# Prefix log-sum-exp: single-row-block tiles at the two ends of the run, each in a loop of its own

## The chip, the cores and the metric

The kernel runs on one core of one Trainium2 chip. The metric is the device time of that core in microseconds, the median of several runs. A ratio is the mean time of one kernel's runs over that of the kernel before in the same rounds, so it is not quite the ratio of the medians quoted beside it.

## The reference

```python
def reference(x):                       # x: (4, 4096, 4128) float32
    out = np.zeros_like(x)
    out[:, 0, :] = x[:, 0, :].copy()
    for t in range(1, S):
        mx = np.maximum(out[:, t - 1, :], x[:, t, :])
        out[:, t, :] = mx + np.log(np.exp(out[:, t - 1, :] - mx) + np.exp(x[:, t, :] - mx))
    return out.astype(np.float32)
```

It is a running log-sum-exp along the second axis. The kernel computes it as Ln of a running sum of Exp.

## The kernel before

A **block** is 128 rows of 4128 columns, 2.114 MB. Each batch has 32 blocks. A **step** loads up to R = 3 blocks into one of four buffers, sums them in place and stores them from the same buffer. `b` counts the batches.

```python
    steps = []
    for b in range(B):
        n = S // P
        parts = [R] * (n // R) + ([n % R] if n % R else [])
        if b == 0:
            parts.reverse()
        # ... one Step per entry of parts

    chunks = [Chunk(s, c) for s in steps for c in range(n_main)]
    ahead = bufs - 1
    for s in steps[:ahead]:
        s.load()
```

Each step is four chunks of 1024 columns. For each chunk ScalarE (ACT) takes Exp, VectorE (DVE) adds the blocks of the step to each other (`own`), TensorE multiplies by a triangular matrix for the rows above (`head`), VectorE adds that from PSUM (`add_above`), TensorE carries the last row on (`pick`), and ScalarE takes Ln. One software-pipelined loop goes over all chunks of all steps; the Exp runs two chunks ahead, across the border between steps:

```python
    chunks[0].act(ACT.Exp)
    chunks[1].act(ACT.Exp)
    # ...
    for g, k in enumerate(chunks):
        if g + 1 < len(chunks):
            chunks[g + 1].own()
            chunks[g + 1].head()
        if g + 2 < len(chunks):
            chunks[g + 2].act(ACT.Exp)
        if g:
            finish(chunks[g - 1])
            result(chunks[g - 1])      # Ln; after the last chunk: store, and load step stored+3
        k.add_above()
        # ... pick
```

The softmax here doesn't subtract the row's maximum and nothing guards it: scores larger than these inputs give would overflow.

Of the kernel before, what the change touches and what calls it, by code (L numbers as in the profile page):

```python
# [1 line left out]

# [4 lines left out]

FP32 = mybir.dt.float32
ACT = mybir.ActivationFunctionType
P = 128  # L10
R = 3
CH = 1024
MM = 512


def _constants(nc, pool):

    excl = pool.tile([P, P], FP32, name="excl")
    nc.gpsimd.memset(excl, 1.0)  # L19

    nc.gpsimd.affine_select(  # L21
        out=excl, in_=excl, pattern=[[1, P]], compare_op=mybir.AluOpType.is_ge,
        fill=0.0, base=-1, channel_multiplier=-1,
    )
    pick = pool.tile([P, P], FP32, name="pick")
    nc.gpsimd.memset(pick, 0.0)  # L26
    nc.gpsimd.affine_select(  # L27
        out=pick, in_=pick, pattern=[[0, P]], compare_op=mybir.AluOpType.not_equal,
        fill=1.0, base=-(P - 1), channel_multiplier=1,
    )  # L30
    return excl, pick


@with_exitstack
def kernel(
    ctx: ExitStack,
    tc: tile.TileContext,
    x: bass.AP,
    out: bass.AP,
):  # L40







    nc = tc.nc
    B, S, D = x.shape
    assert S % P == 0  # L50
    n_main = D // CH
    tail = D - n_main * CH
    t0 = n_main * CH
    last = n_main - 1

    nc.scalar.preload_act_table_set("natural_log_exp_and_others")  # L56
    consts = ctx.enter_context(tc.tile_pool(name="consts", bufs=1))
    excl, pick = _constants(nc, consts)

    bufs = 4  # L60
    xpool = ctx.enter_context(tc.tile_pool(name="xpool", bufs=bufs))
    cpool = ctx.enter_context(tc.tile_pool(name="cpool", bufs=1))
    psum = ctx.enter_context(tc.tile_pool(name="psum", bufs=1, space=bass.MemoryType.PSUM))

    above = [psum.tile([P, CH], FP32, name=f"above{c}") for c in range(n_main)]

    above_t = above[last][:, CH - MM:CH - MM + tail]
    carry_t = cpool.tile([P, tail], FP32, name="carry_t")
    nc.vector.memset(carry_t, 0.0)  # L69

    ctx.enter_context(tc.manual_schedule())

    def mm(pt, w, rhs, start=False, stop=False):
        nc.tensor.matmul(pt, lhsT=w, rhs=rhs, start=start, stop=stop, skip_group_check=True)  # L74

    def add(o, a, b):
        nc.vector.tensor_tensor(out=o, in0=a, in1=b, op=mybir.AluOpType.add)  # L77

    class Step:


        def __init__(self, b, row, r):
            self.b, self.row, self.r = b, row, r
            self.first = row == 0
            self.final = row + P * r == S

        def dram(self, t):
            rows = t[self.b, self.row:self.row + P * self.r, :]
            return rows.rearrange("(p j) d -> p j d", j=self.r)

        def load(self):
            full = xpool.tile([P, R, D], FP32, name="xt")
            self.xt = full[:, :self.r, :]
            nc.sync.dma_start(out=self.xt, in_=self.dram(x))  # L94

        def store(self):
            nc.sync.dma_start(out=self.dram(out), in_=self.xt)  # L97

    class Chunk:
        def __init__(self, step, c):  # L100
            self.t, self.c = step, c
            self.a, self.b = c * CH, D if c == last else (c + 1) * CH

        def act(self, func):
            v = self.t.xt[:, :, self.a:self.b]
            nc.scalar.activation(v, v, func)  # L106

        def own(self):

            x = self.t.xt  # L110
            for j in range(1, self.t.r):
                v = x[:, j, self.a:self.b]
                add(v, x[:, j - 1, self.a:self.b], v)

        def head(self):

            t, a = self.t, self.a
            for s in range(0, CH, MM):
                mm(above[self.c][:, s:s + MM], excl, t.xt[:, t.r - 1, a + s:a + s + MM],
                   start=t.first, stop=True)  # L120

        def add_above(self):
            t, a = self.t, self.a
            v = t.xt[:, :, a:a + CH]
            add(v, v, above[self.c].unsqueeze(1).to_broadcast([P, t.r, CH]))

        def pick(self, s0=0, s1=CH):

            t, a = self.t, self.a
            if not t.final:  # L130
                for s in range(s0, s1, MM):
                    mm(above[self.c][:, s:s + MM], pick, t.xt[:, t.r - 1, a + s:a + s + MM],
                       start=True)

        def tail_head(self):
            t = self.t
            if not t.first:
                mm(above_t, pick, carry_t, start=True)
            mm(above_t, excl, t.xt[:, t.r - 1, t0:D], start=t.first, stop=True)

        def tail_add(self):
            t = self.t
            v = t.xt[:, :, t0:D]
            add(v, v, above_t.unsqueeze(1).to_broadcast([P, t.r, tail]))
            if not t.final:
                nc.vector.tensor_copy(carry_t[96:, :], t.xt[96:, t.r - 1, t0:D])  # L146

    steps = []
    for b in range(B):
        n = S // P  # L150
        parts = [R] * (n // R) + ([n % R] if n % R else [])
        if b == 0:
            parts.reverse()
        row = 0
        for r in parts:
            steps.append(Step(b, row, r))
            row += P * r
        assert row == S

    chunks = [Chunk(s, c) for s in steps for c in range(n_main)]  # L160
    ahead = bufs - 1
    for s in steps[:ahead]:
        s.load()
    stored = 0
    def finish(k):
        if k.c == last:
            k.tail_add()
            k.pick(CH - MM)

    def result(k):  # L170
        nonlocal stored
        k.act(ACT.Ln)
        if k.c == last:
            k.t.store()
            if stored + ahead < len(steps):
                steps[stored + ahead].load()
            stored += 1

    chunks[0].act(ACT.Exp)
    chunks[1].act(ACT.Exp)  # L180
    chunks[0].own()
    chunks[0].head()
    for g, k in enumerate(chunks):
        if g + 1 < len(chunks):
            chunks[g + 1].own()
            chunks[g + 1].head()
        if g + 2 < len(chunks):
            chunks[g + 2].act(ACT.Exp)
        if g:
            finish(chunks[g - 1])  # L190
            result(chunks[g - 1])
        k.add_above()
        if k.c == last:
            k.tail_head()
            k.pick(0, CH - MM)
        else:
            k.pick()
    finish(chunks[-1])
    result(chunks[-1])


# [1 line left out]
_INS = ['x']  # L203
_OUTS = [((4, 4096, 4128), 'float32')]


# [23 lines left out]
```

## Time and profile before

| | before |
|---|---|
| median time | 1265.1 us (4 runs, 1263.9 to 1265.9) |
| span of the profiled run | 1266.3 us |
| steps, loads, stores | 44, 44, 44 |
| bytes moved | 541.07 MB: 256 blocks, 128 in and 128 out |
| DMA queue / DVE / ACT / PE busy | 99.3% / 77% / 73% / 60% |

The page gives each engine's busy time and share, then strips of 40 equal slices; in the DMA strip a 9 is 90% or more. The prediction below shows the page's lines, the start of the queue and single transfers. Two more lines of the kernel before matter, from the timeline of its end. The columns are start, length of the merged group, engine, line, operation, data, count, and the idle time ahead of it with its cause.

```profile
1218.60 33.39 SPq L97 DMA_DIRECT2D out_dram<-xt  x3
1226.15 20.85 ACT L106 ACTIVATE xt<-xt 128x2048 f32<-128x2048 f32 x10 [2.19 <-DMA xt<-in_x_dram]
```

The last three stores go out between 1218.6 and 1252. From 1226 us on ACT has the four Exps of the last step, with three Lns of the step before it between them, and then three of the last step's own Lns, ten in one unbroken run: that is the streaming which the change gives up at the ends.

### The profile page before, as it was taken

The numbers are of one execution on the slowest core, as the hardware profiler recorded it, in microseconds if no ns is written. First come the engines' busy times: TensorE is split into PE (matmuls) and PEld (weight loads), VectorE is DVE, ScalarE is ACT, GpSimd is POOL, SyncE is SP. The second block draws the span as 40 slices with busy tenths as digits, with TensorE's granted clock in tenths as the row PEclk, the third lists the DMA queues.
The fourth block names the chain that finished last, engine by engine and source line by source line (L and its number), as shares of the span: only waits on it lengthen the run. The fifth ranks groups of instructions, "written<-read, shape, count | busy, mean of one in ns | idle before, by whom it ended". The sixth has DMA issues, their size and how long they took to land.

```text
span 1266.3 us, 4623 instructions
## 1 busy us (share of the span) xinstructions
PE 760.5 (60%) x1512; PEld 289.0 (23%) x1512; DVE 980.6 (77%) x597; ACT 923.8 (73%) x353; POOL 1.1 (0%) x8
## 2 busy tenths in 40 slices
PE   4676665555666666666366666665646656666562
PEld 1222222222222222222122222222212222222220
DVE  3998777777777878788579878777857978787793
ACT  4887666777777777767668777666866877766794
POOL 0000000000000000000000000000000000000000
PEclk9998888887788888888779888888877988888886
DMA  9999999999999999999999999999999999999998
GB/s 409 384 425 424 427 429 443 426 427 440 432 429 441 426 430 440 429 431 433 434 434 434 429 440 430 431 437 433 432 419 434 426 433 433 431 432 438 426 418 349
DMA packets 12695, 541.35 MB, mean 427 GB/s; under 512 B 1409, under 2 KB 1409, under 8 KB 1409
## 3 DMA queue, kind: packets, MB, share of 16 engines
q1 hardware_dynamic: 12672, 541.07, 99.3%
q8 instruction: 12, 0.20, 0.1%
q14 instruction: 11, 0.08, 0.0%
HBM read 270.53 MB, written 270.53 MB: 427 GB/s over the span
## 4 chain that ended last, share of the span: by engine, by line
DMA 67%; DVE 12%; ACT 9%; PE 8%; issue 1%; SPq 0%; ACTq 0%
DMA xt<-in_x_dram 63%; DVE xt L77 12%; ACT xt L106 9%; PE above L74 8%; DMA out_dram<-xt 5%; SPq L97 0%; ACTq L106 0%; SPq L94 0%; DVE carry_t L146 0%
## 5 line engine op out<-in xcount | busy, mean ns | idle before, releaser
L106 ACT ACTIVATE xt<-xt 128x3072 f32<-128x3072 f32 (+2 forms) x352 | 922.5, 2693 | 327.0 <-DMA xt<-in_x_dram 290.5
L74 PE MATMUL above<-xt,excl 128*128 128x512 f32 (+1 forms) x792 | 443.1, 687 | 348.7 <-DVE xt L77 339.4
L77 DVE TENSOR_TENSOR xt<-xt 128x1024 f32<-128x1024 f32 (+1 forms) x336 | 413.4, 1230 | 255.0 <-ACT xt L106 249.4
L77 DVE TENSOR_TENSOR xt<-xt,above 128x3072 f32<-128x3072 f32 (+3 forms) x220 | 582.9, 2651 | 11.7 <-PE above L74 10.3
L74 PE MATMUL above<-xt,pick 128*128 128x512 f32 x640 | 330.7, 630 | 130.0 <-DVE xt L77 130.0
L74 PEld LDWEIGHTS above<-xt,excl 128*128 128x128 f32 x792 | 162.6, 229 | 601.5 <-issue 490.5
L74 PEld LDWEIGHTS above<-xt,pick 128*128 128x128 f32 x640 | 113.6, 198 | 307.4 <-DVE xt L77 227.2
L74 PEld LDWEIGHTS above<-carry_t,pick 128*128 128x128 f32 x80 | 20.8, 271 | 51.4 <-DVE xt L77 48.2
L74 PE MATMUL above<-carry_t,pick 128*128 128x32 f32 x80 | 17.5, 308 | 10.1 <-DVE xt L77 10.1
L146 DVE COPY carry_t<-xt 32x32 f32<-32x32 f32 x40 | 7.1, 178 | 1.4
L56 ACT ACT_TABLE_LOAD x1 | 1.3, 1283 | 0.8 <-PEq L214 0.8
L69 DVE MEMSET carry_t<- 128x32 f32 x1 | 0.1, 85 | 0.9 <-PEq L214 0.9
L27 POOL TENSOR_SCALAR_AFFINE_SELECT pick<-pick 128x128 f32<-128x128 f32 x1 | 0.3, 293 | 0.0
L21 POOL TENSOR_SCALAR_AFFINE_SELECT excl<-excl 128x128 f32<-128x128 f32 x1 | 0.3, 292 | 0.0
L19 POOL MEMSET excl<- 128x128 f32 x1 | 0.2, 204 | 0.3 <-POOLq L214 0.3
L26 POOL MEMSET pick<- 128x128 f32 x1 | 0.2, 204 | 0.0
L214 POOL MEMSET const-bfloat16-1.0<- 128x1 bf16 x1 | 0.1, 101 | 0.0
L214 POOL MEMSET const-uint8-127<- 128x1 uint8 x1 | 0.1, 101 | 0.0
L214 POOL MEMSET const-float32-0.0<- 128x1 f32 x1 | 0.1, 98 | 0.3 <-issue 0.3
L214 POOL MEMSET const-float32-1.0<- 128x1 f32 x1 | 0.1, 98 | 0.0
## 6 DMA issues: line engine op xcount, KB each, us to landing
xt<-in_x_dram SPq DMA_DIRECT2D x40, 6192.0 KB, 41.1
out_dram<-xt SPq DMA_DIRECT2D x40, 6192.0 KB, 27.0
xt<-in_x_dram SPq DMA_DIRECT2D x4, 4128.0 KB, 36.2
out_dram<-xt SPq DMA_DIRECT2D x4, 4128.0 KB, 19.6
```

Of the source, the lines that this page charges most:

```text
L19: nc.gpsimd.memset(excl, 1.0)
L21: nc.gpsimd.affine_select(out=excl, in_=excl, pattern=[[1, P]], compare_op=mybir.AluOpType.is_ge, fill=0.0, base=-1, channel_multiplier=-1,)
L26: nc.gpsimd.memset(pick, 0.0)
L27: nc.gpsimd.affine_select(out=pick, in_=pick, pattern=[[0, P]], compare_op=mybir.AluOpType.not_equal, fill=1.0, base=-(P - 1), channel_mul ...
L56: nc.scalar.preload_act_table_set("natural_log_exp_and_others")
L69: nc.vector.memset(carry_t, 0.0)
L74: nc.tensor.matmul(pt, lhsT=w, rhs=rhs, start=start, stop=stop, skip_group_check=True)
L77: nc.vector.tensor_tensor(out=o, in0=a, in1=b, op=mybir.AluOpType.add)
L106: nc.scalar.activation(v, v, func)
L146: nc.vector.tensor_copy(carry_t[96:, :], t.xt[96:, t.r - 1, t0:D])
L214: nc = _bacc.Bacc("TRN2", target_bir_lowering=False, num_devices=1)
```

## The change

The intent is to let the run begin and end with a small tile: one block first, one block last, with the first and last step in loops of their own. The first batch becomes 1, 3x10, 1 (it was 2, 3x10), and the last 3x10, 1, 1 (it was 3x10, 2).

```diff
-        parts = [R] * (n // R) + ([n % R] if n % R else [])
-        if b == 0:
-            parts.reverse()
+
+        parts = [R] * (n // R)
+        if b == 0 and n % R:
+            parts = [1] + parts + [1] * (n % R - 1)
+        elif b == B - 1:
+            parts = parts + [1] * (n % R)
+        elif n % R:
+            parts = parts + [n % R]
...
-    chunks = [Chunk(s, c) for s in steps for c in range(n_main)]
...
+    for part in (steps[:1], steps[1:-1], steps[-1:]):
+        chunks = [Chunk(s, c) for s in part for c in range(n_main)]
+        # the same loop body as before, one level deeper
```

More of the change, by code (lines that the diff above doesn't have):

```diff
@@ L177, in result @@
             stored += 1
-    chunks[0].act(ACT.Exp)
-    chunks[1].act(ACT.Exp)
-    chunks[0].own()
-    chunks[0].head()
-    for g, k in enumerate(chunks):
-        if g + 1 < len(chunks):
-            chunks[g + 1].own()
-            chunks[g + 1].head()
-        if g + 2 < len(chunks):
-            chunks[g + 2].act(ACT.Exp)
-        if g:
-            finish(chunks[g - 1])
-            result(chunks[g - 1])
-        k.add_above()
-        if k.c == last:
-            k.tail_head()
-            k.pick(0, CH - MM)
-        else:
-            k.pick()
-    finish(chunks[-1])
-    result(chunks[-1])
+    for part in (steps[:1], steps[1:-1], steps[-1:]):
+        chunks = [Chunk(s, c) for s in part for c in range(n_main)]
+        chunks[0].act(ACT.Exp)
+        chunks[1].act(ACT.Exp)
+        chunks[0].own()
+        chunks[0].head()
+        for g, k in enumerate(chunks):
+            if g + 1 < len(chunks):
+                chunks[g + 1].own()
+                chunks[g + 1].head()
+            if g + 2 < len(chunks):
+                chunks[g + 2].act(ACT.Exp)
+            if g:
+                finish(chunks[g - 1])
+                result(chunks[g - 1])
+            k.add_above()
+            if k.c == last:
+                k.tail_head()
+                k.pick(0, CH - MM)
+            else:
+                k.pick()
+        finish(chunks[-1])
+        result(chunks[-1])
 _INS = ['x']
```

## The prediction

> **What bounds the kernel now.** I read the page first (strips, queue share), then the SyncE timeline, then the issue view one transfer at a time.
>
> ```profile
> span 1266.3 us, 4623 instructions
> PE 760.5 (60%) x1512; PEld 289.0 (23%) x1512; DVE 980.6 (77%) x597; ACT 923.8 (73%) x353; POOL 1.1 (0%) x8
> DMA  9999999999999999999999999999999999999998
> GB/s 409 384 425 424 427 429 443 426 427 440 432 429 441 426 430 440 429 431 433 434 434 434 429 440 430 431 437 433 432 419 434 426 433 433 431 432 438 426 418 349
> q1 hardware_dynamic: 12672, 541.07, 99.3%
> ```
>
> The transfers are the bound: one queue is busy 99.3% of the span, while the busiest engine, DVE, has 77%. The strip of GB/s sags only in the first two slices and the last: a few us are all that ordering can win.
>
> ```profile
> 0.80 1.33 SPq L94 DMA_DIRECT2D xt<-in_x_dram  x3
> 42.64 0.35 SPq L97 DMA_DIRECT2D out_dram<-xt  x1
> 43.03 0.43 SPq L94 DMA_DIRECT2D xt<-in_x_dram  x1
> 68.38 0.34 SPq L97 DMA_DIRECT2D out_dram<-xt  x1
> 68.82 0.38 SPq L94 DMA_DIRECT2D xt<-in_x_dram  x1
> 92.60 0.34 SPq L97 DMA_DIRECT2D out_dram<-xt  x1
> ```
>
> These are the issues at the start: three loads at once, then a store and a load per step (a store at L97 waits for the step's last Ln). The next lines are answers of the issue view for single transfers: the first store, then the first full-size store and load after it.
>
> ```profile
> out_dram<-xt SPq DMA_DIRECT2D x1, 4128.0 KB, 12.2
> out_dram<-xt SPq DMA_DIRECT2D x1, 6192.0 KB, 17.9
> xt<-in_x_dram SPq DMA_DIRECT2D x1, 6192.0 KB, 34.3
> ```
>
> Issue plus time to landing gives a chain of landings. The first loads land at 13.1, 27.7 and 42.5 us, so three row blocks cost 14.65 us, **one block 4.88 us**, if the queue is never dry. The first store is issued at 42.64, when the last of those loads has just landed, and takes 12.2 instead of 2 x 4.88 = 9.8: **a dry queue costs about 2.4 us**. The load behind it lands at 69.5 (14.7 later, no loss), the second store at 86.3 and its load at 103.1 (16.8 each: 2.1 lost twice, as the store came at 68.38, only 1.1 us before the queue ran dry). From the fifth store on, stores come every 29.4 us and a load lands 41.5 us after issue: at each store some 12 us of work is queued. A load's landing is followed 16.9 us later by the store of the step before it (landing 1201.7, store 1218.6). At the end the last two stores are issued at 1239.7 and 1251.65 and land at 1255.7 and 1265.6; the transfer before them landed at 1240.7, so the end loses less than 1 us now.
>
> **What the Trainium skill says.**
> - "DMA: Bandwidth & Descriptors", section Bandwidth, gives a fabric ceiling of 435 GB/s for a core's 16 engines. A block is 2.114 MB, so 4.88 us is 433 GB/s: the trace agrees, and there is no faster steady state to reach.
> - Same page, "Anatomy of one DMA": about 2.0 us fixed per transfer (fitted on the GpSimd path), mostly the receipt of the last byte. The 2.4 us of a dry queue agrees; it is hidden while others are queued.
> - "TensorE: Matmul & The Clock Gate", Part 1: the array runs at half clock until about 3.4 us of activity. The first matmuls here step at 0.85 us against 0.43 later: the trace agrees.
> - Same page, queue depths: ScalarE and VectorE are strict FIFO. Hence an Exp of the next step that waits for its load holds back the Ln of this one; the first ACT wait at 27.7 us shows it.
>
> **The change part by part.**
>
> Steps: before 2,3x10 | 3x10,2 | 3x10,2 | 3x10,2 (44). After 1,3x10,1 | 3x10,2 | 3x10,2 | 3x10,1,1 (46). Bytes are the same; four more transfers of 4.88 us, hidden when queued. The first and last step are each their own loop, so the engines fill and drain there.
>
> *Start.* Three loads now bring 7 blocks, landing at 8.2, 22.9 and 37.6 us (3.35 us of lead-in from 13.1 - 9.8, then 4.88 per block). Step 0 alone: an Exp of 1024 columns is about 0.98 us (1.90 for 2048 and 2.75 for 3072 give 0.85 per 1024), an add with PSUM 1.22 (3.35 and 2.28 give 1.07 per 1024). TensorE orders it: four heads and four picks of four 0.43 us passes, 8 x 1.72 = 13.8, plus 1.7 cold and 0.9 for the tail: from 9.2 to 25.5, Ln to about 26.5. So store 0 and load 3 go out at 26.5, 16 us sooner, with the queue still full: **the dry spot at 42.6 goes away** (-2.4). Load 3 lands at 37.6 + 4.9 + 14.65 = 57.2.
>
> Then the catch. Step 1 starts on ACT at 26.5 instead of 27.7: Exp 2.75, two own-sums of 2.5 each with the second hidden behind a cold head of 3.4, so its first add with PSUM is near 35 instead of 37.98. From that add to the store it was 68.38 - 37.98 = 30.4, four DVE rounds of 5.66 and the tail, so store 1 comes at **about 65**, only 3.4 us sooner, while the queue ran dry at 57.2, 12.3 us sooner than 69.5. Store 1 lands at 65 + 2.4 + 14.65 = 82 with 14 blocks done; before, 86.3 with 16. Two blocks are 9.8: **5.5 us behind**. Starting from a really dry queue, the load behind may not lose its 2.1 again, so I count 4.5.
>
> *Middle.* The 1-block step at the end of batch 0 makes one supply 4 blocks (19.5 us) where stores come 29.3 apart, so the backlog falls from 12 to 12.4 + 19.5 - 29.3 = 2.6 us once, and once more when that step is stored. The old 2-block steps fall to 7.6 and lose nothing. At a backlog of 1.1 a loss of 2.1 was seen, at 2.6 I count **1 us** in all.
>
> *End.* Count from the store that issues the last 3-block load (before: 1159.86, span ends 105.7 later). Backlog 12.4 + 29.3 = 41.7. The next store at 29.2 adds 3 + 1 blocks, to 61.2; the next at 41.7 + 16.7 = 58.4 adds 3 + 1, to 80.7. The last 3-block store follows some 20.5 us later (21.1 before), at 79, to 95.4; the next-to-last block about 10 later (6 PE passes of 1.72 groups, tail, Ln), at 89, to 100.3. Only then does the last step begin its Exp: 0.98 + four heads 6.9 + add 1.2 + tail 1.2 + Ln 1.0 = 11.5 and up to 1.7 more if the PE clock has dropped: store at 101.5 to 103. The queue is dry at 100.3, so it lands at 102 + 2.4 + 4.9 = 109.5 instead of 105.7: **about 4 us behind**. Its data had landed at 80.7, so that is the cost of not streaming.
>
> *Sum.* 1265.8 + 4.5 + 1 + 4 = about 1275; I say 1274, as some of the dry spots overlap with receipts already paid.
>
> **The rivals.**
> 1. *The short ends win as intended.* A smaller first load and last store shorten fill and drain: -2.4 at the start, and a last store of 1 block instead of 2 saves 4.9 if nothing else binds: about 1259. For: the low first and last slices. Against: at the end the queue is already nearly full up to the last byte, and fewer blocks in the first three loads leave less to do until store 1, which DVE sets.
> 2. *All is hidden:* the backlog of 12 us swallows both, 1264 to 1268. For: 99.3% busy. Against: no backlog exists near the start and end.
> 3. *The drains hit in full:* fill and drain of engines, some 17 us each, appear whole in the span, 1290 to 1300. For: step 1's Exp stands behind step 0's last Ln. Against: its data lands only 3.6 us before that Ln ends, and the queue holds work through both.
>
> **Range and chances.** Rival 1 sets the low side only partly; the restarts at low backlog (0 to 2 us each, four places) the high side: 1266 to 1282. Faster by 2% needs under 1240.5, while 256 blocks at 4.88 are 1249 alone: 1%. Slower by 2% needs over 1291: only rival 3, 3%. Within 2%: 96%.
>
> **What would show it.** First store near 26.5, second near 65 with a gap in transfers between about 57 and 66; no gap at 42; last store issued some 12 us after the one before, behind a short gap; GB/s of slice 2 below 384, steady slices unchanged near 432; DVE and ACT busy up by a few us. I am wrong if store 1 comes before 60, if the last store is issued within 10 us of the one before it, or if steady slices change.

## The result

The changed kernel takes **1279.8 us** in the median (4 runs, 1277.8 to 1282.4) against 1265.1, a ratio of 1.0118 (95% interval 1.0097 to 1.0139): 14.7 us slower, within the 2% that counts as the same. From the page of its profile:

```profile
span 1280.6 us, 4817 instructions
PE 787.9 (62%) x1584; PEld 302.5 (24%) x1584; DVE 973.8 (76%) x601; ACT 926.8 (72%) x369; POOL 1.1 (0%) x8
DMA  9799999999999999999999999999999999999998
GB/s 413 314 395 420 424 441 429 436 426 413 415 418 421 421 443 423 443 423 438 432 431 438 426 443 424 439 427 438 431 421 431 435 421 432 435 432 435 432 381 373
q1 hardware_dynamic: 13248, 541.07, 98.6%
```

The bytes are the same and no engine's work grew by more than PE's 27 us (72 matmuls more, for two steps more). The new spots are slices 2 and 3, with 314 and 395 GB/s instead of 384 and 425, slices 10 to 14 (the end of the first batch), with 413 to 421 instead of 426 to 441, and slice 39, with 381 instead of 418. The SyncE timeline of the start, as the prediction shows it of before:

```profile
0.80 1.33 SPq L94 DMA_DIRECT2D xt<-in_x_dram  x3
28.36 0.35 SPq L97 DMA_DIRECT2D out_dram<-xt  x1
28.75 0.43 SPq L94 DMA_DIRECT2D xt<-in_x_dram  x1
66.11 0.34 SPq L97 DMA_DIRECT2D out_dram<-xt  x1
66.55 0.38 SPq L94 DMA_DIRECT2D xt<-in_x_dram  x1
90.94 0.34 SPq L97 DMA_DIRECT2D out_dram<-xt  x1
```

The first store comes 14 us sooner (28.4 for 42.6), the second only 2.3 us sooner (66.1 for 68.4). In between, 11 blocks were all that the queue was given. The stretches view of those us (window, length, busy us and instructions of PE, PEld, DVE, ACT and POOL, the granted PE clock, the DMA share, GB/s) shows the hole:

```profile
58.50:66.50 8.00, 5.73 (x13) 1.87 (x12) 7.87 (x8) 4.40 (x3) 0.00 (x0) 1.00 0.00 0
```

For 8 us no transfer moves a byte, and DVE is busy for 7.87 of them: it works on step 1. The issue view of the second store and of the load behind it gives the landings, 83.1 and 101.2 us:

```profile
out_dram<-xt SPq DMA_DIRECT2D x1, 6192.0 KB, 17.0
xt<-in_x_dram SPq DMA_DIRECT2D x1, 6192.0 KB, 34.6
```

Three blocks cost 14.65 us in a full queue. The store takes 17.0, so 2.4 more; the load lands 18.1 after it, so 3.4 more again. What holds step 1 is seen in the timeline of the start:

```profile
27.26 11.78 ACT L106 ACTIVATE xt<-xt 128x1056 f32<-128x1056 f32 x5 [1.48 <-PE above L74]
31.02 2.48 DVE L77 TENSOR_TENSOR xt<-xt 128x1024 f32<-128x1024 f32 x2 [4.82 <-ACT xt L106]
37.40 3.35 DVE L77 TENSOR_TENSOR xt<-xt,above 128x3072 f32<-128x3072 f32 x1 [1.24 <-PE above L74]
```

The group at 27.26 begins with the last Ln of step 0, and the first Exp of step 1 follows it, although its data landed at 23 us. DVE's first add for step 1 is at 37.40, against 37.98 before.

To add up the whole run I use one measure: the **lateness** of a landing, its time minus 4.883 us (14.65 / 3) for each block landed until then (issue time plus time to landing, for each transfer). A full queue keeps it nearly constant; any dry spot raises it. Both profiled runs are 2.6 to 3.0 us above their kernel's median, so their difference can stand for that of the medians.

| at | before | after | difference | grown there |
|---|---|---|---|---|
| load 4 landed (19 and 17 blocks) | 103.1 - 92.8 = 10.3 | 101.2 - 83.0 = 18.2 | 7.9 | start 7.9 |
| 88 blocks | 442.1 - 429.7 = 12.4 | 453.3 - 429.7 = 23.6 | 11.2 | end of batch 0: 3.3 |
| last load landed (248 and 251 blocks) | 1226.1 - 1211.0 = 15.1 | 1253.7 - 1225.6 = 28.1 | 13.0 | rest of the middle: 1.8, of it 0.9 at the last load |
| last store landed (256) | 1265.5 - 1250.0 = 15.5 | 1279.5 - 1250.0 = 29.5 | 14.0 | end 1.0 |

One profile each is a thin base for such a split. Of the kernels below, end-only and doubled begin exactly as the kernel before, and stand at 8.9 and 8.6 at load 4, where it has 10.3; start-only and removed begin as the changed one, and stand at 16.1 and 16.8 where it has 18.2. So the start costs some 6 to 9 us; the means, 17.0 and 9.3, give 7.7.

Over half of the loss is in the first 100 us and little at the end, where the new serial step is plain to see in the timeline:

```profile
1250.48 23.11 SPq L97 DMA_DIRECT2D out_dram<-xt  x3
1258.91 4.89 ACT L106 ACTIVATE xt<-xt 128x1056 f32<-128x1056 f32 x5 [1.70 <-PE above L74]
1260.99 8.83 PE L74 MATMUL above<-xt,excl 128*128 128x512 f32 x16 [2.17 <-ACT xt L106]
1272.15 1.08 ACT L106 ACTIVATE xt<-xt 128x1056 f32<-128x1056 f32 x1 [1.63 <-DVE xt L77]
```

The last step's Exps stand behind the Ln of the step before it at 1258.9, and its last Ln ends at 1273.2. The store before it goes out at 1260.0 and lands at 1273.3, the last one goes out at 1273.3 and lands at 1279.5. The 13.3 us of serial work on the last step are hidden by the transfers that are still queued; only the 1.4 us by which the last landing exceeds a block's 4.9 are open.

### The profile page after: what moved, and what is told of

Its sections match the earlier page's. It is cut to its first block, busy times and chain, and to the rows that moved or that the text cites. A ratio compares the mean times of both kernels' runs of the same rounds, so it can differ in the third digit from the quotient of the medians.

```text
span 1280.6 us, 4817 instructions
## 1 busy us (share of the span) xinstructions
PE 787.9 (62%) x1584; PEld 302.5 (24%) x1584; DVE 973.8 (76%) x601; ACT 926.8 (72%) x369; POOL 1.1 (0%) x8
## 4 chain that ended last, share of the span: by engine, by line
DMA 64%; DVE 13%; PE 13%; ACT 8%; issue 1%; SPq 0%; ACTq 0%; DVEq 0%
DMA xt<-in_x_dram 61%; DVE xt L77 13%; PE above L74 13%; ACT xt L106 8%; DMA out_dram<-xt 4%; SPq L97 0%; DVE carry_t L146 0%; ACTq L106 0%; SPq L94 0%; DVEq L77 0%
## 5 line engine op out<-in xcount | busy, mean ns | idle before, releaser
L106 ACT ACTIVATE xt<-xt 128x3072 f32<-128x3072 f32 (+4 forms) x368 | 925.5, 2585 | 345.6 <-DMA xt<-in_x_dram 277.6
L74 PE MATMUL above<-xt,excl 128*128 128x512 f32 (+1 forms) x828 | 454.2, 676 | 336.6 <-DVE xt L77 307.9
L77 DVE TENSOR_TENSOR xt<-xt,above 128x3072 f32<-128x3072 f32 (+4 forms) x230 | 584.4, 2543 | 52.8 <-PE above L74 51.4
L77 DVE TENSOR_TENSOR xt<-xt 128x1024 f32<-128x1024 f32 (+1 forms) x328 | 403.7, 1231 | 243.2 <-ACT xt L106 237.7
L74 PE MATMUL above<-xt,pick 128*128 128x512 f32 x672 | 348.4, 632 | 137.4 <-DVE xt L77 137.4
L74 PEld LDWEIGHTS above<-xt,excl 128*128 128x128 f32 x828 | 169.9, 228 | 597.1 <-issue 489.6
L74 PEld LDWEIGHTS above<-xt,pick 128*128 128x128 f32 x672 | 119.0, 197 | 320.8 <-DVE xt L77 236.9
L74 PE MATMUL above<-carry_t,pick 128*128 128x32 f32 x84 | 18.2, 306 | 9.9 <-DVE xt L77 9.9
```

Source lines behind the costliest of these rows:

```text
L74: nc.tensor.matmul(pt, lhsT=w, rhs=rhs, start=start, stop=stop, skip_group_check=True)
L77: nc.vector.tensor_tensor(out=o, in0=a, in1=b, op=mybir.AluOpType.add)
L106: nc.scalar.activation(v, v, func)
```

## The experiments

**Theory A:** a store that comes after the queue has run dry is what costs. At the start there are too few blocks to last until store 1; in the middle a single-block step supplies too little; at the end the last step is serial. **Theory B:** the drains of the engines between the three loops cost. Two finer rivals come up below: **B2**, that the serial last step is the greater part, and **F**, that the late landings in the middle are instruction fetches. Kernels sent together shared the chip and the runs of the kernel before, whose median was 1264.6 to 1264.8 us; each experiment has 4 to 6 runs.

### Row blocks only

```diff
+        parts = [R] * (n // R)
+        if b == 0 and n % R:
+            parts = [1] + parts + [1] * (n % R - 1)
+        elif b == B - 1:
+            parts = parts + [1] * (n % R)
+        elif n % R:
+            parts = parts + [n % R]
     # the single streamed loop of the kernel before
```

> The new row blocks (1, 3x10, 1 in the first batch; 3x10, 1, 1 in the last), but one streamed loop over all steps as in the kernel before. Theory A (too few blocks at the start, single-block steps in the middle that let the queue run low, and a serial last step): only the fill of step 1 and the last step get better than in the changed kernel, so store 1 comes near 63.5 us instead of 66.1, its transfer still waits in a queue dry since 58, the middle loses its 5 us as before, and the end loses under 1 us. About 10 us over the kernel before, some 1275 us, ratio 1.007 to 1.010. Theory B (the split of the loop is the cost): within 3 us of the kernel before, ratio under 1.003.

Measured: 1277.4 us, ratio 1.0100 (1.0085 to 1.0116), at the upper edge of what Theory A said. The SyncE timeline of its start:

```profile
38.06 0.35 SPq L97 DMA_DIRECT2D out_dram<-xt  x1
63.38 0.34 SPq L97 DMA_DIRECT2D out_dram<-xt  x1
```

Store 1 comes at 63.4, where Theory A put it at 63.5. Load 3 had landed at 60.0; store 1 lands 5.8 us late. After 20 blocks the lateness is 14.5, against 10.4 before (after 22 blocks) and 18.1 in the changed kernel (after 20): the blocks alone bring 4.1 of the start's loss. The middle loses what it lost in the changed kernel: 1.7 us at load 12 and 1.6 at load 15. At the end, streamed here, the last store loses nothing. Theory B, which allowed a ratio under 1.003, falls.

### Split only

```diff
+    for part in (steps[:1], steps[1:-1], steps[-1:]):
     # the row blocks of the kernel before: 2, 3x10 | 3x10, 2 | ...
```

> The row blocks of the kernel before (2 first, 2 last), but the first and last step each in a loop of their own. Theory A: store 0 near 35 us with the queue still full, store 1 near 73 instead of 68.4, into a queue dry since 67; the last store about 16.5 us after the one before it instead of 11.9. Some 3 to 5 us lost at the start and 3 at the end: about 1272 us, ratio 1.004 to 1.007, and nothing lost in the middle. Theory B: nearly all of the change's 14 us, ratio 1.009 or more.

Measured: 1276.0 us, ratio 1.0090 (1.0076 to 1.0104). This is a miss: Theory A said at most 1.007, and the value stands at the lower edge of what B said. Its timeline shows why:

```profile
37.06 0.35 SPq L97 DMA_DIRECT2D out_dram<-xt  x1
74.63 0.34 SPq L97 DMA_DIRECT2D out_dram<-xt  x1
```

Store 1 comes at 74.6 (73 was expected) and load 3 had landed at 67.8. It lands 10.2 us late, and the next two loads add 1.8 and 1.2; after 25 blocks the lateness is 17.5, against 10.5 before: 7.0 at the start, with 3 to 5 expected. I had taken what follows a dry spot as no worse than in the kernel before. Nothing is lost in the middle, as expected: from there to the last load it grows by 1.5, less than before. The end costs more than the 3 us expected. The transfer before the last store lands at 1259.4, but the serial last step, of two blocks here, issues its store only at 1262.7:

```profile
1241.54 0.34 SPq L97 DMA_DIRECT2D out_dram<-xt  x1
1262.66 0.33 SPq L97 DMA_DIRECT2D out_dram<-xt  x1
```

The queue is dry for 3.3 us and the last landing is 4.6 late, against 0.4 for the last two stores of the kernel before. So a last step of one block makes the serial end cheaper, though not free. At the start each half of the change delays store 1 against the supply, and the two together (7.9) cost much less than their sum (4.1 + 7.0): there both act through one event, not through separate costs.

### Start only

```diff
         parts = [R] * (n // R) + ([n % R] if n % R else [])
         if b == 0:
-            parts.reverse()
+            parts = [1] + [R] * (n // R) + [1] * (n % R - 1)
+    for part in (steps[:1], steps[1:]):
```

> First batch as in the changed kernel (1, 3x10, 1) with the first step in its own loop; last batch and last step as before. Theory A: the first-step loss of 8 us and the middle loss of 3 to 5 us are both here, the end as in the kernel before: ratio 1.009 to 1.011, some 1278 us; store 1 near 66 us. Theory B2 (the serial last step is the greater part): ratio under 1.005.

Measured: 1280.3 us, ratio 1.0121 (1.0104 to 1.0138), a little above what was expected and the same as the whole change. The change to the first batch alone brings the whole loss, and Theory B2 falls.

### End only

```diff
+        elif b == B - 1:
+            parts = [R] * (n // R) + [1] * (n % R)
+    for part in (steps[:-1], steps[-1:]):
```

> First batch as before; last batch 3x10, 1, 1 with the last step in its own loop. Theory A: the transfers ran dry for only 1.4 us before the last store of the changed kernel, so 1 to 2.5 us over the kernel before, ratio 1.001 to 1.002. Theory B2: 4 us or more, as I first predicted, ratio 1.003 or more.

Measured: 1266.4 us, ratio 1.0015 (0.9999 to 1.0030). The single-block end with its serial last step costs 2 us or nothing; the size agrees with Theory A, though the interval just touches no cost and just touches 4 us. Its trace has the loss where Theory A puts it: the last store is issued at 1257.4, 0.8 us after the transfer before it has landed, and its own landing is 2.2 us late.

### A single-block step in the middle, doubled and removed

Doubled, in the kernel before:

```diff
+        elif b == 1:
+            parts = [R] * (n // R) + [1] * (n % R)      # 3x10, 1, 1 in place of 3x10, 2
```

> The kernel before, with the 2-block step that ends its second batch cut into two of 1 block; start, end and loop untouched. Theory M (a single-block load adds 4 blocks of transfers in a period of 6, so the backlog of the slowest of the 16 engines falls to 2 to 3 us and the other engines, which are 4 to 5 us ahead of it, run dry): 3 to 6 us lost, ratio 1.002 to 1.005, shown as landings that are late by over 1 us about the end of the second batch. Theory F (the late landings in the middle of the changed kernel are instruction fetches that hit one engine, as they do in the kernel before): within 1.5 us of before, ratio under 1.0015.

Removed, in the changed kernel:

```diff
-            parts = [1] + parts + [1] * (n % R - 1)
+            parts = [1] + [R] * (n // R - 1) + [2, 2]
```

> The changed kernel with its first batch cut as 1, 9x3, 2, 2: the single-block step at the end of the first batch is gone, first and last step stay as the change has them. Theory M: backlog no lower than 7 us, so 3 to 5 us come back: about 1275 us, ratio 1.007 to 1.009 to the kernel before. Theory F: as the changed kernel, ratio 1.011 to 1.012.

Measured: doubled 1273.8 us, ratio 1.0072 (1.0059 to 1.0084), more than the 1.002 to 1.005 expected. Removed 1275.3 us, ratio 1.0086 (1.0074 to 1.0098), within the expected range, and 4.5 us below the changed kernel's median of the earlier rounds (4.0 by the two ratios). Theory F, which wanted under 1.0015 and at least 1.011, fails both tests. The cost was underestimated where both single-block steps lie in a row, as the SyncE timeline and the issue view of the doubled kernel show for the store that followed them:

```profile
681.88 0.34 SPq L97 DMA_DIRECT2D out_dram<-xt  x1
out_dram<-xt SPq DMA_DIRECT2D x1, 6192.0 KB, 18.0
```

The transfer before it landed at 682.3, so the backlog was 0.4 us; it took 18.0 and landed at 699.9, 2.9 late, and the load behind it 1.7 more. Over blocks 119 to 149 the lateness grew from 9.9 to 19.0 us.

Why a backlog of nearly 3 us was not enough in the changed kernel is read from the 16 completion updates that each transfer leaves in the trace. There are 16 DMA engines, and I take the updates as one from each. They do not say which engine they come from, so "median" and "last" are places in their order, and can be other engines from one transfer to the next. At the end of its first batch, in us from the span's start, and worked out by sorting those updates:

```
transfer            median engine   last engine   last minus first   since the transfer before: median, last
load 11 (1 block)       293.9          297.0            3.8                    4.8,  4.9
store 9 (3 blocks)      311.0          311.6            1.0                   17.0, 14.6
load 12 (3 blocks)      326.9          327.9            1.4                   15.9, 16.2
```

Store 9 was issued at 294.3. By the last engine there were 2.7 us of work left; the median engine had already finished, at 293.9, and its next transfer took 17.0 instead of 14.65. It lost 2.4 us, of which it was without work for 0.4 before the issue. The last engine lost nothing there, but its next transfer took 16.2, and with that the whole queue was late.

The same reading of other stores gives one rule for these kernels. The median engine had been without work for 8.5 us at store 1 of the changed kernel, and lost 10.5. It had 1.2 us left at store 12, and lost 1.0. At store 1 of the kernel before it had 1.0 left, and lost 1.1. So a store with a load behind it loses about 2 us less what the median engine has left when it is issued. A last store, with no load behind it, loses less: in the split-only kernel it found the median engine without work for 5.2 us and lost 6.4.

### Steps of two blocks, streamed (e6) and split

```diff
-R = 3
+R = 2
-    bufs = 4
+    bufs = 6
```

> The kernel before with steps of 2 blocks and 6 buffers in place of 3 and 4 (the same bytes of SBUF), all streamed. Theory A (what the start loses is the queue running dry before the second store): five loads of 2 blocks last until 52 us, store 0 comes near 35 and store 1 near 50, the queue is never dry, and the 7 us that the kernel before loses in its first 100 us come back: about 1259 us, ratio 0.994 to 0.997. Rival: more transfers and more instruction fetches on the queue eat it: ratio 0.998 or more.

> As e6, with the changed kernel's three loops: with steps of 2 blocks all batches divide evenly, so the split of the first and last step is the only thing that is left of the change. Theory A: with five loads ahead the drain after step 0 falls into a full queue and costs nothing at the start; the last step alone costs some 3 us, as its store comes 16 us after the one before it: 2 to 4 us over e6. Theory B (a drain of the engines costs its own length wherever it is): 7 us or more over e6, as the split alone cost over the kernel before with 2-block ends.

Measured: streamed 1264.4 us, ratio 0.9997 (0.9985 to 1.0009); split 1264.4 us, ratio 0.9996 (0.9983 to 1.0009). The split costs **nothing** that can be measured here (each interval is 1.5 us to either side), neither at the start nor at the end, where I had expected some 3 us. From the SyncE timeline of the split kernel:

```profile
37.03 0.35 SPq L97 DMA_DIRECT2D out_dram<-xt  x1
62.80 0.34 SPq L97 DMA_DIRECT2D out_dram<-xt  x1
```

Store 1 comes nearly 9 us later than in the streamed one (53.97), but five loads and store 0 keep the queue at work until 62.9, and the load behind them until 74.5. Theory B is wrong in the clearest way: the same drains are there, and are free when the queue is deep.

The other half of the expectation failed: the streamed kernel was to gain some 5 us and gains none. Its start is as good as expected, a lateness of 6.6 after 28 blocks against 10.6 before, but it creeps to 11.3 by the last load: 4.7 more, where the end-only kernel, with the start of the kernel before, gained 1.9 from block 34 to its last load. At its last store the first of the 16 engines is done 8.9 us before the last one, the median one 5.8 us before it. In the kernel before the engines' spread fell from 6.3 to 0.2 us at the last store but one, which met a nearly dry queue; this queue is never dry, and so nothing evens the spread out. The rival of my expectation fits the sign: 128 transfers and 6426 instructions against 88 and 4623. That it is fetches or transfer count which hold one engine back is argued, not shown.

### A ramp at the start

```diff
         if b == 0:
-            parts.reverse()
+            parts = [1, 2] + [R] * (n // R - 1) + [2]
```

> The kernel before, streamed as it is, with its first batch cut as 1, 2, 9x3, 2 in place of 2, 10x3. Theory A (a store must come before the queue runs dry; small steps bring the first stores sooner, but what was loaded ahead must last until the next): three loads of 6 blocks last until 32.6 us; store 0 near 29, store 1 near 46 with the queue full until 52, store 2 near 68 with it full until 76, so no dry spot at all, and the 4 to 6 us that the kernel before loses by its two dry spots mostly come back: about 1261 us, ratio 0.996 to 0.998. If store 0 comes after 32.6, or the single-block step brings the backlog under 3 us, it is 1264 or more, ratio 1.000 and above.

Measured: 1262.2 us, ratio 0.9981 (0.9967 to 0.9995), faster than both kernels, by a little: 2.6 us of the 4 to 6 hoped for, just outside the expected ratio. The SyncE timeline of its stores:

```profile
30.18 0.35 SPq L97 DMA_DIRECT2D out_dram<-xt  x1
48.60 0.34 SPq L97 DMA_DIRECT2D out_dram<-xt  x1
72.64 0.34 SPq L97 DMA_DIRECT2D out_dram<-xt  x1
```

The transfers before these three landed at about 33, at 52.6 and at 77.3, so each store came in time. From the page's strips:

```profile
GB/s 403 428 430 438 433 433 428 431 435 437 427 438 428 431 435 440 428 431 434 429 437 434 437 431 430 434 439 428 436 425 434 434 434 436 430 433 434 435 427 345
```

Slice 2 has 428 GB/s, where the kernel before has 384 and the changed one 314. After 18 blocks the lateness is 4.8 us, a full queue nearly from the first byte. It, too, begins with a single-block step, so the smallness of the first tile is not what hurts: what hurts is what comes behind it.

## Why the prediction was right or wrong

The direction and the mechanism were right, and 1279.8 is inside 1266 to 1282, though the point, 1274, was 6 us short. That it was no shorter is in part luck: the start and the middle were put 5.7 us too low together, and the end too high. By its own steps:

- **The bound and the price of a block: right.** The middle slices stay near 432 GB/s, and 4.88 us per block fits the full stretches of all runs. Rivals 1 to 3 are out: 1259, 1264 to 1268 and 1290 to 1300 were all missed, and the run with deep prefetch shows the drains hidden, where rival 3 had them in full.
- **Store 0 near 26.5, store 1 near 65: right in kind,** 28.4 and 66.1 measured. The gap at 42 us went, and a new one came from 58.5 to 66.5. The second time is so close because two errors offset each other: the first add of step 1 came at 37.4, not near 35, and from it to the store it was 28.7 us, not 30.4.
- **"The load behind may not lose its 2.1 again, so I count 4.5": wrong.** Store 1 landed 6.6 behind (83.1 plus 9.8 for two blocks, minus 86.3; 5.5 predicted), and the load behind it lost not 0 but 3.4, against 2.2 before. The start's term is 7.9. This discount is one of the two steps that failed: it followed load 3, which lost nothing behind a 2-block store into a dry queue, and set aside load 4, which had lost behind a full-size store.
- **"At a backlog of 1.1 a loss of 2.1 was seen, at 2.6 I count 1 us in all": wrong.** The places were right (at the step's load and at its store), the size was 3.3 us by 88 blocks, and removing the step brought 4.0 to 4.5 back. The backlog had been counted to the landing of a transfer, which is that of its last engine; the median engine was 3.0 us ahead of it at store 9 and had run dry, and 1.6 ahead at store 12, with 1.2 us left.
- **"About 4 us behind" at the end: wrong in size.** The serial chain was right (the last store 101.6 us after the store I counted from; predicted 101.5 to 103), but the queue did not end at 100.3. It ran until 101.6, as the transfers were themselves late by then. So the last stores cost 1.0. Another 0.9 was lost at the last load, behind a store that met a backlog of 2.6 after the one-block load of the new end. Together that is the 1.9 us of the run with the end alone.
- **The remaining 0.9 us** grew slowly over the other batches. Single profiles of other kernels differ by as much there; I do not assign it.
- **"DVE and ACT busy up by a few us": half wrong.** ACT rose by 3.0; DVE fell by 6.8. A single-block step has no blocks to add to each other, so eight own-sums of 1.23 us are gone; the two added steps' other adds and copies give part of that back.
- **Slips that changed nothing.** The third load landed at 42.3, not 42.5 (it was issued at 1.71 and took 40.6 us). The "four more transfers of 4.88 us" move no more blocks than before, and no such term is in the sum. The ACT wait that ends at 27.7 is no witness for an Exp holding an Ln back, as TensorE still worked on the next Ln's chunk until 28.0. The wait of 7.4 us that ends at 1201.7 is one: the Ln behind that Exp had its chunk by 1194.6 and began at 1204.4.

What stays open: why the load behind a store that met a dry queue is slow itself, by 1.1 to 3.4 us where the store was of full size, and not after the 2-block first store of the kernel before or the 1-block one of the row-blocks kernel. The experiments show it each time and do not say why. The completion updates split it: of the 3.4 us in the changed kernel the median engine loses 1.3, and it loses 1.1 to 1.4 in the four other kernels with such a start; the rest, 2.1, is the last engine falling behind the others.

## What to carry to other kernels

In a kernel bound by transfers, ask of every store when it is issued and when the queue would run dry without it; the work between them is free if the store comes some 2 us before that point, the time after is lost, and a transfer or two behind it can be slow as well. A small first tile helps only if what was loaded beside it lasts until the next store: a ramp of 1, 2, 3 did it here, 1 followed by 3 did the opposite. Count the backlog to the median DMA engine, not to a transfer's landing.

## What the Trainium skill lacked or had wrong

- "DMA: Bandwidth & Descriptors", Bandwidth: its warning there says that for transfers between HBM and SBUF the HBM side, some 358 GB/s, binds. On this single core a stream of half loads and half stores held 431 GB/s for over 1100 us, near the fabric ceiling of 435 in the same section, and far over 358. The page's own 425 GB/s for 16 MB points the same way, and its note on that table gives the condition that the warning lacks: some 358 for each core when both cores of the HBM domain stream. No run here has a second core.
- Same page, "Anatomy of one DMA": the fixed 2.0 us is given per transfer, fitted on the GpSimd path. On the SyncE queue a store into a dry queue cost 2.4 us, which fits; what the page lacks is that a store loses already when the median engine has less than about 2 us left (1.0 lost with 1.2 left), and that the load behind it can lose as well (1.1 to 3.4 us).
- Same page, "Why a DMA increments its semaphore by 16 and not by 1": it says that the engines finish independently, but gives no size. In a stream on one queue the first and last engine of a transfer were 3.8 us apart after 290 us in the changed kernel. At 1200 us it was 4.5 to 7.0 in the kernels with steps of up to three blocks, and at the last store 8.9 to 10.1 in the two with steps of two. A landing therefore overstates the backlog.
